# Three MLP chunks with summed weights: the engines' order written down in the source, the next item but one split into the buffers of the running one

## The chip, the cores and the metric

The kernel runs on one core of a Trainium2 chip. The metric is the device time of one execution in microseconds, the median of several runs; lower is better. Engine names are those of the profile: PE is TensorE (matmuls), PEld its weight loads, ACT is ScalarE, DVE is VectorE, SP issues the loads.

## The reference

One decoder layer on 256 tokens of width 2048: a recurrent branch and a windowed attention branch, an output projection, then a squared-ReLU MLP and a final norm. The change lies in the MLP alone:

```python
h2 = _modulate(_rms_norm(x, norm2_g[l]), shift2, scale2)
ff = jnp.square(jax.nn.relu(jnp.einsum("bsd,df->bsf", h2, w_ff1[l])))      # 2048 -> 8192
x = x + gate2[:, None, :] * jnp.einsum("bsf,fd->bsd", ff, w_ff2[l])        # 8192 -> 2048
return _rms_norm(x, final_g)
```

Inputs and outputs are float32.

## The kernel before

**Split operands.** Each matmul operand is held as a rounded part and a rest (`wh` and `wl` for weights), and three matmuls (wh by both parts of the activations, wl by the rounded part) stand for one product. A weight tile of 1 MB arrives in a buffer `raw` (in the profile `rw`); ACT rounds it into `wh` (`w_round`, L178) and DVE subtracts (`w_rest`, L183) into `wl`, in two pieces of 1024 columns. There are four `raw` buffers, four of `wh` and four of `wl`. So two items (a running one and the next) fill `wh` and `wl`, and the pieces of the next but one can only go where the running item's pieces were.

**Four chunks.** The hidden width of 8192 is cut in four chunks c = 0 to 3 of 16 tiles. In chunks 1 to 3, with which the change deals, three kinds of item follow each other on PE:

- **F items** (`ff1_unit`), 16 to a chunk: 48 matmuls of 128x256 (L204 to L206) into half of a PSUM bank; two F items that follow each other share a bank (`half_of`), from the fifth on. Then ACT applies relu (L1099), square (L1103) and rounds the result (L166), and DVE subtracts the rest (L167).
- **S items** (`sum_step`), 16 to a chunk: 21 matmuls (L1033 to L1035). They work out eight tiles of the second layer with 7 products of sums in the place of 8, as in Strassen's scheme. Their left side is a pair of F results and sums of its four blocks (`token_sums`: DVE L978 to L981 for every second F, then ACT L983 and DVE L984). Their right side is made by `weight_sums`: two loads (L991, 512 KB in all), three DVE sums in the same buffer (L993, L996, L997), and the same rounding and subtracting in pieces of 1024 and 768 columns.
- **G items** (`ff2_unit`): the other eight tiles of the second layer. Tiles 8 to 11 have 48 narrow matmuls into half banks; DVE adds each to the residual (L1209). Tiles 12 to 15 use a wide form (L229 and L230).

PE's order in such a chunk is F0 F1 F2 F3 S0 F4 S1 F5 ... F15 S12 G8 S13 G9 S14 G10 S15 G11 G12 and so on. During S14 and S15 the seven banks of the products become complete, and `sums_out` copies them out (c = 1, ACT L1008) or adds them to what the chunk before left (c = 2 and 3, DVE L1010). At the end of chunk 3 the products are joined (L1049), transposed back (L1056) and added to the residual.

**What sets the order.** A loop over all units asks, ahead of unit n, for loads and splits up to unit n + 2, then runs unit n. A scheduler turns that into the order on each engine while it builds the program; only instructions that are wrapped in `pin` keep the order of the source. Before the change, nothing of chunks 1 to 3 is pinned but the last two G tiles. Each engine works off its instructions in the order so made: one that waits holds back all behind it.

Of the kernel before, what the change touches and what calls it, by code (L numbers as in the profile page):

```python
# [10 lines left out]
F32 = mybir.dt.float32  # L11
# [6 lines left out]
P = 128  # L18
T = 256
# [47 lines left out]
def hybrid_layer(ctx: ExitStack, tc: tile.TileContext, x, xt, wada, w_p, w_r, w_f, vec, lruw, relb,  # L67
# [108 lines left out]
    def w_round(raw, o, c, pin=lambda i: i):  # L176
        wh = wp.tile([P, WCH], F32R, tag="wh", name=nm("wh"), bufs=WH_BUFS)
        pin(se.activation(wh[:, :c], raw[:, o:o + c], AF.Copy))  # L178
        return wh

    def w_rest(raw, o, c, wh, pin=lambda i: i):
        wl = wp.tile([P, WCH], F32R, tag="wl", name=nm("wl"), bufs=WH_BUFS)
        pin(ve.tensor_tensor(out=wl[:, :c], in0=raw[:, o:o + c], in1=wh[:, :c].bitcast(F32), op=ALU.subtract))  # L183
        return wh, wl
# [789 lines left out]
    def token_sums(p):  # L974
        a, b = sq.pop(2 * p), sq.pop(2 * p + 1)
        a11, a21, a12, a22 = a[:, :P], a[:, P:], b[:, :P], b[:, P:]
        s = tmp([P, 4, P])
        ve.scalar_tensor_tensor(out=s[:, 0], in0=a21, scalar=-1.0, in1=a22, op0=ALU.mult, op1=ALU.subtract)  # L978
        ve.scalar_tensor_tensor(out=s[:, 1], in0=s[:, 0], scalar=-1.0, in1=a11, op0=ALU.mult, op1=ALU.subtract)
        ve.tensor_tensor(out=s[:, 2], in0=a11, in1=a21, op=ALU.subtract)  # L980
        ve.tensor_tensor(out=s[:, 3], in0=a12, in1=s[:, 1], op=ALU.subtract)  # L981
        hi, lo = (kp.tile([P, 4, P], F32R, tag="k2", name=nm("ts")) for _ in range(2))
        se.activation(hi, s, AF.Copy)  # L983
        ve.tensor_tensor(out=lo, in0=s, in1=hi.bitcast(F32), op=ALU.subtract)  # L984
        ts[p] = hi, lo

    def weight_sums(u, p):
        raw = wp.tile([P, 8, T], F32, tag="raw", name=nm("rw"), bufs=RAW_BUFS)
        for k in range(2):
            e = (2 * p + k) * P  # L990
            nc.sync.dma_start(out=raw[:, 2 * k:2 * k + 2].rearrange("p a (b m) -> p (a b) m", m=P),  # L991
                              in_=w_f[u:u + SUMMED, :, e:e + P].rearrange("u p m -> p u m"))
        ve.tensor_tensor(out=raw[:, 4:6], in0=raw[:, 1:3], in1=raw[:, 0:1].broadcast_to((P, 2, T)), op=ALU.subtract)  # L993
        flat = raw.rearrange("p a b -> p (a b)")
        parts = [w_rest(flat, T, 4 * T, w_round(flat, T, 4 * T))]
        ve.tensor_tensor(out=raw[:, 6], in0=raw[:, 2], in1=raw[:, 4], op=ALU.add)  # L996
        ve.tensor_tensor(out=raw[:, 7], in0=raw[:, 6], in1=raw[:, 3], op=ALU.subtract)  # L997
        return parts + [w_rest(flat, 5 * T, 3 * T, w_round(flat, 5 * T, 3 * T))]

    yt = []  # L1000

# [15 lines left out]
    def sum_step(c, p, u, q):  # L1017
        def run(w):
            if p == 0 and q == 0:
                pq[0] = [bank([P, 2, T]) for _ in range(4)]  # L1020
                pq[0] += [pg.tile([P, 2, T], F32, tag="pg", name=nm("pg")) for _ in range(7 * QUADS // 2 - 4)]
            hi, lo = ts[p]
            fa, fb = ff[c, 2 * p], ff[c, 2 * p + 1]
            own = lambda f, t: (f[:, 0, t * P:(t + 1) * P], f[:, 1, t * P:(t + 1) * P])
            of = lambda i: (hi[:, i], lo[:, i])
            prods = ((own(fa, 0), 0, 0), (own(fb, 0), 0, 2), (of(3), 0, 1), (of(0), 0, 3),
                     (of(2), 1, 0), (of(1), 1, 1), (own(fb, 1), 1, 2))
            for n, ((xh, xl), i, o) in enumerate(prods, 7 * q):
# [4 lines left out]
                te.matmul(ps, lhsT=xh, rhs=wh[:, e], start=p == 0 and n % 2 == 0, stop=False)  # L1033
                te.matmul(ps, lhsT=xh, rhs=wl[:, e], start=False, stop=False)
                te.matmul(ps, lhsT=xl, rhs=wh[:, e], start=False, stop=end)  # L1035
# [4 lines left out]
        add_unit(run, lambda: weight_sums(u, p), 1024)  # L1040

    def joined(q, i):
        return yt[(7 * q + i) // 2][:, (7 * q + i) % 2]
# [27 lines left out]
    def half_of(f, own=False):  # L1071
        if own or f % 2 == 0:
            hb[0] = pg.tile([P, 2, T], F32, tag="pg", name=nm("pg"))
        return hb[0][:, f % 2]

    def ff1_unit(c, f):
        def run_first(w):
            ps = pg.tile([P, 258], F32, tag="pg", name=nm("pg"))
            for k in range(KT):
                wh, wl = w[k * P // WCH]  # L1080
                e = slice(k * P % WCH, k * P % WCH + P)
                te.matmul(ps, lhsT=wh[:, e], rhs=z[k][:, 0:258], start=k == 0, stop=False)  # L1082
# [12 lines left out]

        def run(w):
            t = tmp()
            if c >= SUMMED_FROM:
                se.activation(t[:, 0], gemm(w, 0, [zn[k] for k in range(KT)], half_of(f, f < 4)), AF.Relu)  # L1099
            else:  # L1100
                gemm_wide(w, [zn[k] for k in range(KT)], out=t[:, 0])
                se.activation(t[:, 0], t[:, 0], AF.Relu)
            se.activation(t[:, 1], t[:, 0], AF.Square)  # L1103
            ff[c, f] = split(t[:, 1])
            if c >= SUMMED_FROM:
                sq[f] = t[:, 1]
                if f % 2 == 1:
                    token_sums(f // 2)
        add_unit(run_first if c == 0 and f < ZN_FROM else run)

    def rest_part(f, w, acts):
# [81 lines left out]
    def ff2_unit(c, f):  # L1193
        def run(w):
            if c == 3 and f >= 14:
                held.append(w)
                if f == 15:
                    last_units(*held)
                return
            if c == 0:  # L1200
                flush(5 * KT + f + 1)
            acts = [ff[c, j] for j in range(16)]
            if c >= SUMMED_FROM and f < SUMMED * QUADS + 4:
                pss = [gemm(w, 0, acts, half_of(f))]
            else:
                ps = gemm_wide(w, acts, join=False)
                pss = [ps[:, 0], ps[:, 1]]
            for ps in pss:
                ve.scalar_tensor_tensor(out=x1[f], in0=ps, scalar=mod[:, 5 * KT + f:5 * KT + f + 1], in1=x1[f],  # L1209
                                        op0=ALU.mult, op1=ALU.add)  # L1210
# [28 lines left out]
    for c in range(4):  # L1239
        summed = SUMMED * QUADS if c >= SUMMED_FROM else 0  # L1240
        u2 = full[0] + 16
        steps = [(p, u2 + q * SUMMED, q) for p in range(KT // 2) for q in range(QUADS)] if summed else []
        for f in range(16):
            ff1_unit(c, f)
            if f > 2 and steps:
                sum_step(c, *steps.pop(0))
        full[0] += summed
        for f in range(summed, 16):
            ff2_unit(c, f)
            if steps:  # L1250
                sum_step(c, *steps.pop(0))

    ready, credit, ada_credit = {0: split_w.pop(len(p_units))}, 0.0, 0.0
    for n, (run, src, size) in enumerate(units):
        if n == ATT:
            stage[0] = pin
            attention(ready)
            stage[0] = same
        if ATT <= n < ATT + 2 * GROUPS:
            continue  # L1260
        left = n_z - n
        if n < n_ya:
# [116 lines left out]
```

## Time and profile before

| | |
|---|---|
| median of 3 runs | 1571.03 us (1569.51 to 1571.73) |
| the profiled execution: its time | 1570.03 us |
| its span | 1568.2 us |
| DVE busy in the span | 1302.1 us (83%) |
| ACT busy in the span | 923.7 us (59%) |
| relu of the 48 F items (L1099), first and last start | 1015.5 and 1499.0 us |

Times inside the span count from its start. The profile's parts that are used below are: the busy time of each engine in stretches of the span, with instruction counts in brackets; the list of waits (who waited, for whom, total us, times, longest); and the timeline (start, us, engine, line, operation, with the idle time ahead of it and what ended it in square brackets). An instruction may start a little ahead of the end of the one in front of it, so the distance between two starts, not the duration, is what an engine pays for it in a dense queue.

### The profile page before, as it was taken

To read this page: it belongs to the slowest core of one execution; us is meant where nothing else is said; L and a number is where in the kernel's file an instruction comes from. 1 tells how busy PE (TensorE), PEld (TensorE's weight loads), DVE (VectorE), ACT (ScalarE), POOL (GpSimd) and SP (SyncE) were. 2 spreads that over 40 slices of the span, in tenths; PEclk is the share of its full clock that TensorE was granted. 3 is DMA by queue.
4 is the path that set the end of the run, shared out by engine and by line. 5 is a ranking of instruction groups with operands and counts; after the bars stand their busy time and mean duration, and the time that the engine had idled before them with its cause. 6 is when DMAs were issued, how large, how long until landed. Compare 5 with 4: busy or idle time off the path is not lost.

```text
span 1568.2 us, 28025 instructions
## 1 busy us (share of the span) xinstructions
PE 1541.7 (98%) x11225; PEld 1444.7 (92%) x11225; DVE 1302.1 (83%) x2059; ACT 923.7 (59%) x1517; POOL 0.2 (0%) x4
## 2 busy tenths in 40 slices
PE   8999999999999999999999999999999999999998
PEld 7999999999988888888889988999999999999997
DVE  5898988889899899998898877877776777777887
ACT  5753456667998664444566853465554555456565
POOL 0000000000000000000000000000000000000000
PEclk9999999999999999999999999999999999999999
DMA  9998976665677769888877677845564555645561
GB/s 371 360 377 314 365 286 232 224 233 203 231 257 262 244 242 366 323 298 309 332 274 264 209 263 267 310 161 170 197 230 148 165 184 176 242 146 190 179 221 71
DMA packets 108370, 388.09 MB, mean 247 GB/s; under 512 B 7920, under 2 KB 61520, under 8 KB 69584
## 3 DMA queue, kind: packets, MB, share of 16 engines
q1 hardware_dynamic: 103248, 381.51, 67.7%
q10 hardware_dynamic: 4992, 4.79, 1.0%
q8 instruction: 88, 1.44, 0.4%
q14 instruction: 42, 0.34, 0.1%
HBM read 384.13 MB, written 2.15 MB: 246 GB/s over the span
## 4 chain that ended last, share of the span: by engine, by line
PE 77%; DVE 9%; DMA 8%; ACT 3%; issue 2%; SPq 0%; DVEq 0%; ACTq 0%
PE pg L230 24%; PE pg L229 11%; PE pg L204 10%; PE pg L206 10%; PE pg L205 10%; DMA rw<-in_w_f_dram 7%; DVE wl L183 6%; ACT wh L178 1%; PE pg L1084 1%; PE pg L1083 1%; PE pg L1082 1%; DMA ra<-in_wada_dram 1%; PE pg L232 1%; PE pa L678 1%; PE pa L725 1%
## 5 line engine op out<-in xcount | busy, mean ns | idle before, releaser
L178 ACT ACTIVATE wh<-rw 128x1024 fp32r<-128x1024 f32 (+2 forms) x566 | 575.8, 1029 | 404.4 <-PE pg L230 149.7
L183 DVE TENSOR_TENSOR wl<-rw,wh 128x1024 fp32r<-128x1024 f32 (+2 forms) x566 | 667.6, 1188 | 100.4 <-ACT wh L178 97.2
L230 PE MATMUL pg<-k,wh 128*128 128x512 f32 x1680 | 581.7, 394 | 0.7 <-DVE k L167 0.7
L206 PE MATMUL pg<-k,wl 128*128 128x256 f32 x1838 | 517.2, 282 | 10.1 <-DVE wl L183 9.5
L204 PE MATMUL pg<-k,wh 128*128 128x256 f32 x1838 | 518.9, 282 | 2.1 <-DVE k L1209 2.1
L205 PE MATMUL pg<-k,wh 128*128 128x256 f32 x1838 | 515.3, 280 | 0.0
L229 PE MATMUL pg<-k,wl 128*128 128x256 f32 x1575 | 441.7, 281 | 0.0
L230 PEld LDWEIGHTS pg<-k,wh 128*128 128x128 f32 x1680 | 308.9, 188 | 64.8 <-PE pg L230 0.9
L206 PEld LDWEIGHTS pg<-k,wl 128*128 128x128 f32 x1838 | 346.0, 188 | 14.7 <-DVE wl L183 14.4
L204 PEld LDWEIGHTS pg<-k,wh 128*128 128x128 f32 x1838 | 346.2, 188 | 7.4 <-issue 5.5
L205 PEld LDWEIGHTS pg<-k,wh 128*128 128x128 f32 x1838 | 345.8, 188 | 0.3
L229 PEld LDWEIGHTS pg<-k,wl 128*128 128x128 f32 x1575 | 296.1, 188 | 5.4 <-ACT k L166 0.8
L283 DVE CUSTOM_DVE_ANT_0 ra<-ra,scr,vc 128x2048 f32<-128x2048 f32 x96 | 225.1, 2345 | 10.0 <-DMA ra<-in_wada_dram 8.6
L993 DVE TENSOR_TENSOR rw<-rw 128x512 f32<-128x512 f32 x48 | 33.2, 692 | 86.3 <-DMA rw<-in_w_f_dram 86.3
L983 ACT ACTIVATE ts<-t 128x512 fp32r<-128x512 f32 x24 | 15.2, 634 | 80.8 <-DVE t L981 80.8
L236 ACT ACTIVATE t<-pg 128x256 f32<-128x256 f32 x79 | 28.9, 366 | 24.4 <-PE pg L230 24.4
L686 ACT ACTIVATE t<-t,as 128x128 f32<-128x128 f32 x64 | 28.4, 445 | 22.4 <-DVE as L683 22.4
L1082 PE MATMUL pg<-z,wh 128*128 128x258 f32 x144 | 40.9, 284 | 0.0
L1083 PE MATMUL pg<-z,wh 128*128 128x256 f32 x144 | 40.9, 284 | 0.0
L1084 PE MATMUL pg<-z,wl 128*128 128x258 f32 x144 | 40.7, 283 | 0.0
L1209 DVE SCALAR_TENSOR_TENSOR k<-pg,mod,k 128x256 f32<-128x256 f32 x64 | 30.8, 481 | 10.9 <-PE pg L230 7.6
L167 DVE TENSOR_TENSOR k<-t,k 128x256 fp32r<-128x256 f32 x80 | 33.5, 420 | 3.9 <-ACT k L166 3.9
(237 smaller groups left out, 1636.4 us busy)
## 6 DMA issues: line engine op xcount, KB each, us to landing
rw<-in_w_f_dram SPq DMA_DIRECT2D x176, 1024.0 KB, 5.0
ra<-in_wada_dram SPq DMA_DIRECT2D x96, 1024.0 KB, 6.6
rw<-in_w_r_dram SPq DMA_DIRECT2D x30, 1024.0 KB, 5.2
rw<-in_w_p_dram SPq DMA_DIRECT2D x29, 960.0 KB, 7.1
rw<-in_w_f_dram SPq DMA_DIRECT2D x96, 256.0 KB, 3.2
bt<-ud ACTq DMA_DIRECT2D x8, 512.0 KB, 3.6
k<-in_w_p_dram SPq DMA_DIRECT2D x9, 256.0 KB, 10.8
lw<-in_lruw_dram SPq DMA_DIRECT2D x4, 512.0 KB, 6.2
```

The lines of the kernel that those rows point to most:

```text
L167: pin(ve.tensor_tensor(out=hl[:, 1], in0=src, in1=hl[:, 0].bitcast(F32), op=ALU.subtract))
L178: pin(se.activation(wh[:, :c], raw[:, o:o + c], AF.Copy))
L183: pin(ve.tensor_tensor(out=wl[:, :c], in0=raw[:, o:o + c], in1=wh[:, :c].bitcast(F32), op=ALU.subtract))
L204: pin(te.matmul(ps, lhsT=wh[:, w], rhs=hl[:, 0], start=k == 0, stop=False))
L205: pin(te.matmul(ps, lhsT=wh[:, w], rhs=hl[:, 1], start=False, stop=False))
L206: pin(te.matmul(ps, lhsT=wl[:, w], rhs=hl[:, 0], start=False, stop=k == n - 1))
L229: te.matmul(ps[:, 0], lhsT=wl[:, w], rhs=hl[:, 0], start=False, stop=False)
L230: te.matmul(ps, lhsT=wh[:, w], rhs=hl, start=k == 0, stop=k == n - 1)
L283: pin(ve.tensor_tensor_reduce(out=raw, in0=raw, in1=scr, scale=1.0, scalar=vc[:, V_BADA + c:V_BADA + c + 1], op0=ALU.mult, op1=ALU.add, ac ...
L1082: te.matmul(ps, lhsT=wh[:, e], rhs=z[k][:, 0:258], start=k == 0, stop=False)
L1083: te.matmul(ps[:, 0:256], lhsT=wh[:, e], rhs=z[k][:, 258:514], start=False, stop=False)
L1084: te.matmul(ps, lhsT=wl[:, e], rhs=z[k][:, 0:258], start=False, stop=k == KT - 1)
```

## The change

The order of SP, ACT, DVE and PE in chunks 1 to 3 is written out, from the chunk's first F item to S15, with `pin` around every instruction. Items become objects with `ask` (loads), `sum`, `round` and `rest`, and `mlp` walks over them. While item i runs, item i + 2 is rounded and split (into the buffers that i frees), the sums of an S item at i + 3 are made if i is not an S item, and after it the loads of item i + 6 are asked for. The part of `token_sums` that rounds and splits (`token_parts`) moves behind the splits of the item that follows. What is computed stays the same.

```diff
-    def weight_sums(u, p):
-        raw = wp.tile([P, 8, T], F32, tag="raw", name=nm("rw"), bufs=RAW_BUFS)
-        for k in range(2):
...
-        ve.tensor_tensor(out=raw[:, 4:6], in0=raw[:, 1:3], in1=raw[:, 0:1].broadcast_to((P, 2, T)), op=ALU.subtract)
-        flat = raw.rearrange("p a b -> p (a b)")
-        parts = [w_rest(flat, T, 4 * T, w_round(flat, T, 4 * T))]
-        ve.tensor_tensor(out=raw[:, 6], in0=raw[:, 2], in1=raw[:, 4], op=ALU.add)
-        ve.tensor_tensor(out=raw[:, 7], in0=raw[:, 6], in1=raw[:, 3], op=ALU.subtract)
-        return parts + [w_rest(flat, 5 * T, 3 * T, w_round(flat, 5 * T, 3 * T))]
+    class Item:
...
+        def sum(self):
+            r = self.sums
+            pin(ve.tensor_tensor(out=r[:, 4:6], in0=r[:, 1:3], in1=r[:, 0:1].broadcast_to((P, 2, T)), op=ALU.subtract))
+            pin(ve.tensor_tensor(out=r[:, 6], in0=r[:, 2], in1=r[:, 4], op=ALU.add))
+            pin(ve.tensor_tensor(out=r[:, 7], in0=r[:, 6], in1=r[:, 3], op=ALU.subtract))
...
+    def mlp(items, ready, n):
+        items[0].parts, items[1].parts = ready[n], ready[n + 1]
+        end = len(items) - 2
+        for it in items[2:6]:
+            it.ask()
+        late = []
+        for i, it in enumerate(items[:end]):
+            new, soon = items[i + 2], items[i + 3] if i + 3 < len(items) else None
+            ps = it.run(it.parts)
+            ready[n + i] = it.parts = None
+            new.round()
+            new.rest()
+            if not it.step and soon and soon.step:
+                soon.sum()
+            if not it.step:
+                it.done[0](ps)
+            new.round()
+            if not it.step:
+                it.done[1](ps)
+            new.rest()
+            if not it.step:
+                it.done[2](ps)
+            while late:
+                token_parts(*late.pop(0))
+            if it.done and it.done[3]:
+                late.append((it.done[3][0], token_sums(it.done[3][0])))
+            if i + 6 < len(items):
+                items[i + 6].ask()
...
+    def first_item(c, f):
+        t = {}
+        def relu(ps):
+            t[0] = tmp()
+            pin(se.activation(t[0][:, 0], ps, AF.Relu))
...
+        return Item(run, (relu, square, rest, [f // 2] if f % 2 else None), next_src())
+    def second_item(c, f):
+        def out(ps):
+            pin(ve.scalar_tensor_tensor(out=x1[f], in0=ps, scalar=mod[:, 5 * KT + f:5 * KT + f + 1], in1=x1[f],
+                                        op0=ALU.mult, op1=ALU.add))
...
+        return Item(run, (same, same, out, None), next_src())
...
+        if n in pinned:
+            mlp(pinned[n], ready, n)
-        if ATT <= n < ATT + 2 * GROUPS:
+        if ATT <= n < ATT + 2 * GROUPS or n in inside:
             continue
```

The order on SP is the same before and after, row by row, and so is all that stands ahead of chunk 1 on every engine; PE's differs only in where the transposes of chunk 3 stand. What moves is the order on DVE and ACT in the three chunks.

On DVE, the first place is the alternation of F and S items in chunk 1. The names carry the buffers' numbers: SP loads rw1738, rw1750, rw1758, rw1763, rw1773 in this order (S, F, S, F, S), and with four buffers rw1773 goes where rw1738 was. Before:

```order
L183 TENSOR_TENSOR wl1742_11207<-rw1738_11195,wh1741_11205 128x768
L984 TENSOR_TENSOR ts1737_11192<-t1735_11186,ts1736_11191 128x512
L183 TENSOR_TENSOR wl1752_11241<-rw1750_11237,wh1751_11239 128x1024
L993 TENSOR_TENSOR rw1773_11410<-rw1773_11410 128x512
L183 TENSOR_TENSOR wl1754_11245<-rw1750_11237,wh1753_11243 128x1024
L996 TENSOR_TENSOR rw1773_11410<-rw1773_11410 128x256
L183 TENSOR_TENSOR wl1760_11308<-rw1758_11302,wh1759_11306 128x1024
L167 TENSOR_TENSOR k1757_11299<-t1755_11247,k1757_11299 128x256
L183 TENSOR_TENSOR wl1762_11314<-rw1758_11302,wh1761_11312 128x768
L997 TENSOR_TENSOR rw1773_11410<-rw1773_11410 128x256
L183 TENSOR_TENSOR wl1765_11341<-rw1763_11337,wh1764_11339 128x1024
```

After, at the like place, SP loads rw1711, rw1720, rw1730, rw1739, rw1753 (S, F, S, F, S), and rw1753 goes where rw1711 was:

```order
L183 TENSOR_TENSOR wl1750_11238<-rw1711_10985,wh1749_11236 128x768
L987 TENSOR_TENSOR ts1752_11241<-t1738_11197,ts1751_11240 128x512
L183 TENSOR_TENSOR wl1756_11298<-rw1720_11059,wh1755_11296 128x1024
L1010 TENSOR_TENSOR rw1730_11128<-rw1730_11128 128x512
L1011 TENSOR_TENSOR rw1730_11128<-rw1730_11128 128x256
L1012 TENSOR_TENSOR rw1730_11128<-rw1730_11128 128x256
L183 TENSOR_TENSOR wl1760_11310<-rw1720_11059,wh1758_11305 128x1024
L1146 TENSOR_TENSOR k1759_11307<-t1757_11303,k1759_11307 128x256
L183 TENSOR_TENSOR wl1763_11338<-rw1730_11128,wh1762_11336 128x1024
L183 TENSOR_TENSOR wl1765_11342<-rw1730_11128,wh1764_11340 128x768
L183 TENSOR_TENSOR wl1768_11397<-rw1739_11202,wh1767_11395 128x1024
L1010 TENSOR_TENSOR rw1753_11244<-rw1753_11244 128x512
```

The three sums L993, L996 and L997 are now L1010 to L1012, the rest of `token_sums` L984 is now L987, and L167 of the F results is L1146. Between the last reading of a buffer's old contents and the first sum on what is loaded into it next stood two rows; now ten stand there, and the three sums lie together ahead of their own splits.

The second place is DVE in chunk 2 around the end of G9, whose residual update writes k1335 (L1209, now L1154); `scr` with `pa` is the first addition of finished products (in the source before L1010, now L1063). Before:

```order
L997 TENSOR_TENSOR rw2216_14740<-rw2216_14740 128x256
L183 TENSOR_TENSOR wl2213_14685<-rw2211_14681,wh2212_14683 128x1024
L1209 SCALAR_TENSOR_TENSOR k1335_8614<-pg2205_14596,mod_107,k1335_8614 128x256
L1010 TENSOR_TENSOR scr_104<-pa2025_13310,scr_104 128x512
L183 TENSOR_TENSOR wl2215_14689<-rw2211_14681,wh2214_14687 128x1024
```

After:

```order
L183 TENSOR_TENSOR wl2216_14740<-rw2196_14558,wh2215_14738 128x1024
L1010 TENSOR_TENSOR rw2203_14593<-rw2203_14593 128x512
L1011 TENSOR_TENSOR rw2203_14593<-rw2203_14593 128x256
L1012 TENSOR_TENSOR rw2203_14593<-rw2203_14593 128x256
L1063 TENSOR_TENSOR scr_104<-pa2022_13305,scr_104 128x512
L183 TENSOR_TENSOR wl2218_14747<-rw2196_14558,wh2217_14745 128x1024
L1154 SCALAR_TENSOR_TENSOR k1335_8614<-pg2204_14596,mod_107,k1335_8614 128x256
```

The update of G9 stood ahead of the second split of G10 (rw2211) and of the first addition of products; now it stands behind both (rw2196 is G10's).

More of the change, by code (lines that the diff above doesn't have):

```diff
@@ L977, in token_sums @@
         s = tmp([P, 4, P])
[L978 to L981, printed above, removed]
+        pin(ve.scalar_tensor_tensor(out=s[:, 0], in0=a21, scalar=-1.0, in1=a22, op0=ALU.mult, op1=ALU.subtract))
@@ L982, in token_sums, with token_parts @@
+        pin(ve.scalar_tensor_tensor(out=s[:, 1], in0=s[:, 0], scalar=-1.0, in1=a11, op0=ALU.mult, op1=ALU.subtract))
+        pin(ve.tensor_tensor(out=s[:, 2], in0=a11, in1=a21, op=ALU.subtract))
+        pin(ve.tensor_tensor(out=s[:, 3], in0=a12, in1=s[:, 1], op=ALU.subtract))
+        return s
+    def token_parts(p, s):
         hi, lo = (kp.tile([P, 4, P], F32R, tag="k2", name=nm("ts")) for _ in range(2))
-        se.activation(hi, s, AF.Copy)
-        ve.tensor_tensor(out=lo, in0=s, in1=hi.bitcast(F32), op=ALU.subtract)
+        pin(se.activation(hi, s, AF.Copy))
+        pin(ve.tensor_tensor(out=lo, in0=s, in1=hi.bitcast(F32), op=ALU.subtract))
@@ L985, in token_sums, with __init__, ask, round @@
         ts[p] = hi, lo
-    def weight_sums(u, p):
-        raw = wp.tile([P, 8, T], F32, tag="raw", name=nm("rw"), bufs=RAW_BUFS)
-        for k in range(2):
[L990 to L993, printed above, removed]
-        flat = raw.rearrange("p a b -> p (a b)")
-        parts = [w_rest(flat, T, 4 * T, w_round(flat, T, 4 * T))]
-        ve.tensor_tensor(out=raw[:, 6], in0=raw[:, 2], in1=raw[:, 4], op=ALU.add)
-        ve.tensor_tensor(out=raw[:, 7], in0=raw[:, 6], in1=raw[:, 3], op=ALU.subtract)
-        return parts + [w_rest(flat, 5 * T, 3 * T, w_round(flat, 5 * T, 3 * T))]
+    class Item:
+        def __init__(self, run, done, src=None, u=None, p=None):
+            self.run, self.done, self.src, self.u, self.p = run, done, src, u, p
+            self.step = src is None
+            self.cuts = ((T, 4 * T), (5 * T, 3 * T)) if self.step else ((0, WCH), (WCH, WCH))
+            self.whs, self.parts = [], []
+        def ask(self):
+            if not self.step:
+                self.raw = w_dma(self.src, 2048, pin)[0]
+                return
+            self.sums = wp.tile([P, 8, T], F32, tag="raw", name=nm("rw"), bufs=RAW_BUFS)
+            for k in range(2):
+                e = (2 * self.p + k) * P
+                pin(nc.sync.dma_start(out=self.sums[:, 2 * k:2 * k + 2].rearrange("p a (b m) -> p (a b) m", m=P),
+                                      in_=w_f[self.u:self.u + SUMMED, :, e:e + P].rearrange("u p m -> p u m")))
+            self.raw = self.sums.rearrange("p a b -> p (a b)")
+        def sum(self):
[3 more added lines that the diff above has]
+            pin(ve.tensor_tensor(out=r[:, 7], in0=r[:, 6], in1=r[:, 3], op=ALU.subtract))
+        def round(self):
+            self.whs.append(w_round(self.raw, *self.cuts[len(self.whs)], pin))
+        def rest(self):
+            j = len(self.parts)
+            self.parts.append(w_rest(self.raw, *self.cuts[j], self.whs[j], pin))
@@ new lines, in mlp @@
+    def mlp(items, ready, n):
[26 more added lines that the diff above has]
+                items[i + 6].ask()
+        while late:
+            token_parts(*late.pop(0))
+        ready[n + end], ready[n + end + 1] = items[end].parts, items[end + 1].parts
@@ L1032, in run @@
                 end = p == KT // 2 - 1 and n % 2 == 1
-                te.matmul(ps, lhsT=xh, rhs=wh[:, e], start=p == 0 and n % 2 == 0, stop=False)
-                te.matmul(ps, lhsT=xh, rhs=wl[:, e], start=False, stop=False)
-                te.matmul(ps, lhsT=xl, rhs=wh[:, e], start=False, stop=end)
+                pin(te.matmul(ps, lhsT=xh, rhs=wh[:, e], start=p == 0 and n % 2 == 0, stop=False))
+                pin(te.matmul(ps, lhsT=xh, rhs=wl[:, e], start=False, stop=False))
+                pin(te.matmul(ps, lhsT=xl, rhs=wh[:, e], start=False, stop=end))
             if q == QUADS - 1:
@@ L1039, in run @@
                     sums_out(c)
-        add_unit(run, lambda: weight_sums(u, p), 1024)
+        chunk[-1][1].append(Item(run, None, u=u, p=p))
+        add_unit(run, lambda: None, 1024)
     def joined(q, i):
@@ L1074, in half_of, with square, rest, run @@
         return hb[0][:, f % 2]
+    chunk = []
+    def first_item(c, f):
[3 more added lines that the diff above has]
+            pin(se.activation(t[0][:, 0], ps, AF.Relu))
+        def square(_):
+            hl = ff[c, f] = pair(F32R)
+            pin(se.activation(t[0][:, 1], t[0][:, 0], AF.Square))
+            pin(se.activation(hl[:, 0], t[0][:, 1], AF.Copy))
+        def rest(_):
+            sq[f] = t[0][:, 1]
+            pin(ve.tensor_tensor(out=ff[c, f][:, 1], in0=sq[f], in1=ff[c, f][:, 0].bitcast(F32), op=ALU.subtract))
+        def run(w):
+            return gemm(w, 0, [zn[k] for k in range(KT)], half_of(f, f < 4), pin)
+        return Item(run, (relu, square, rest, [f // 2] if f % 2 else None), next_src())
[3 more added lines that the diff above has]
+                                        op0=ALU.mult, op1=ALU.add))
+            if c == 3:
+                last_square(f)
+        def run(w):
+            return gemm(w, 0, [ff[c, j] for j in range(16)], half_of(f), pin)
+        return Item(run, (same, same, out, None), next_src())
+    def next_src():
+        return w_f[full[0]]
     def ff1_unit(c, f):
@@ L1097, in run @@
             t = tmp()
[L1098 to L1102, printed above, removed]
+            gemm_wide(w, [zn[k] for k in range(KT)], out=t[:, 0])
+            se.activation(t[:, 0], t[:, 0], AF.Relu)
             se.activation(t[:, 1], t[:, 0], AF.Square)
             ff[c, f] = split(t[:, 1])
[L1105 to L1108, printed above, removed]
+        if c >= SUMMED_FROM:
+            chunk[-1][1].append(first_item(c, f))
         add_unit(run_first if c == 0 and f < ZN_FROM else run)
@@ L1212, in run @@
                 last_square(f)
+        if c >= SUMMED_FROM and f < SUMMED * QUADS + 5:
+            chunk[-1][1].append(second_item(c, f))
         add_unit(run)
@@ L1242, in hybrid_layer @@
         steps = [(p, u2 + q * SUMMED, q) for p in range(KT // 2) for q in range(QUADS)] if summed else []
+        if summed:
+            chunk.append((len(units), []))
         for f in range(16):
@@ L1251, in hybrid_layer @@
                 sum_step(c, *steps.pop(0))
+    pinned = dict(chunk)
+    inside = set()
+    for n, items in chunk:
+        inside.update(range(n, n + len(items) - 2))
     ready, credit, ada_credit = {0: split_w.pop(len(p_units))}, 0.0, 0.0
```

## The prediction

> **What bounds the kernel now.** I read the page first, for the span and for PE's share; then the busy times by stretch, to see where PE falls behind its pace; then the waits there; then the timeline, for the loop behind them.
>
> ```profile
> span 1568.2 us, 28025 instructions
> PE 1541.7 (98%) x11225; PEld 1444.7 (92%) x11225; DVE 1302.1 (83%) x2059; ACT 923.7 (59%) x1517; POOL 0.2 (0%) x4
> ...
> rw<-in_w_f_dram SPq DMA_DIRECT2D x176, 1024.0 KB, 5.0
> ```
>
> PE is busy for 98% of the span, so the kernel is bound by PE, and a change of order can win only what PE loses by waiting. Where that is, the stretches show. The first is a stretch of six S and F pairs in chunk 1 that runs smoothly; the others begin where chunks 1, 2 and 3 begin to lose pace, and end with the first matmul after G9.
>
> ```profile
> core 0: us, PE busy (x) PEld busy (x) DVE busy (x) ACT busy (x) POOL busy (x), PEclk, DMA share, GB/s
> 1031.49:1080.45 48.96, 48.96 (x417) 48.96 (x416) 39.43 (x63) 30.26 (x45) 0.00 (x0) 1.00 0.54 175
> 1082.94:1153.06 70.12, 64.74 (x534) 63.18 (x533) 52.96 (x84) 36.73 (x54) 0.00 (x0) 1.00 0.52 169
> 1249.52:1335.78 86.26, 81.99 (x672) 79.80 (x671) 66.59 (x105) 46.87 (x69) 0.00 (x0) 1.00 0.53 174
> 1440.40:1515.68 75.28, 72.78 (x602) 71.35 (x602) 59.20 (x93) 43.28 (x64) 0.00 (x0) 1.00 0.56 180
> ```
>
> The counts hold two or three matmuls that began ahead of the edge. Six pairs are 6 x (48 + 21) = 414 matmuls in 48.96 us, a pace of 0.1183 us, 5.68 us for an F and 2.48 us for an S, 8.16 us a pair. At that pace 531, 669 and 600 matmuls take 62.8, 79.1 and 71.0 us; the stretches took 70.1, 86.3 and 75.3. PE loses 7.3 + 7.1 + 4.3 = **18.7 us** here. The granted clock is 1.00 throughout. More than these 18.7 us the change can't win.
>
> ```profile
> DVE rw L993 <- DMA rw<-in_w_f_dram: 86.3, 45, 4.0
> ...
> PEld pg L206 <- DVE wl L183: 14.4, 22, 1.7
> ```
>
> PE's weight loads wait for the rest `wl` (22 times, 14.4 us; with the slower restarts the larger part of the 18.7), and DVE, which makes it, stands for 86.3 us before the first sum L993 until a load lands. One turn of this:
>
> ```profile
> 1080.05 0.92 SPq L991 DMA_DIRECT2D rw<-in_w_f_dram  x2
> ```
>
> ```profile
> 1085.45 0.69 DVE L993 TENSOR_TENSOR rw<-rw 128x512 f32<-128x512 f32 x1 [3.96 <-DMA rw<-in_w_f_dram]
> 1086.06 1.22 DVE L183 TENSOR_TENSOR wl<-rw,wh 128x1024 fp32r<-128x1024 f32 x1
> 1087.20 0.28 DVE L978 SCALAR_TENSOR_TENSOR t<-t,t 128x128 f32<-128x128 f32 x1
> 1087.40 0.28 DVE L980 TENSOR_TENSOR t<-t 128x128 f32<-128x128 f32 x1
> 1087.60 0.28 DVE L979 SCALAR_TENSOR_TENSOR t<-t,t 128x128 f32<-128x128 f32 x1
> 1087.81 1.22 DVE L183 TENSOR_TENSOR wl<-rw,wh 128x1024 fp32r<-128x1024 f32 x1
> 1088.94 0.42 DVE L167 TENSOR_TENSOR k<-t,k 128x256 fp32r<-128x256 f32 x1
> 1089.28 0.28 DVE L981 TENSOR_TENSOR t<-t,t 128x128 f32<-128x128 f32 x1
> 1089.48 0.95 DVE L183 TENSOR_TENSOR wl<-rw,wh 128x768 fp32r<-128x768 f32 x1
> 1090.35 0.69 DVE L984 TENSOR_TENSOR ts<-t,ts 128x512 fp32r<-128x512 f32 x1
> 1090.95 0.42 DVE L996 TENSOR_TENSOR rw<-rw 128x256 f32<-128x256 f32 x1
> 1091.29 1.22 DVE L183 TENSOR_TENSOR wl<-rw,wh 128x1024 fp32r<-128x1024 f32 x1
> ```
>
> An S buffer is asked for at 1080.05, as soon as it is free; DVE stops at 1085.45 - 3.96 = 1081.49 and holds back two F splits until the load is in, 5.40 us after its issue. Then it works 4.90 us (1085.45 to 1090.35) until the next S buffer is free. 5.4 + 4.9 us is a turn of 10.3 us where the load takes long, against PE's 8.16. In the smooth stretch the loads still run ahead.
>
> **The change, part by part.** Loads, splits, sums and matmuls keep their number and size, so nothing is removed or added but waits.
>
> *The S sums move.* By the order of after, ten DVE rows lie between the freeing of an S buffer and its next first sum, where two did: 0.60 + 1.14 + 1.29 + 1.14 + 0.34 + 1.14 + 0.87 + 1.14 = 7.7 us of work, by the distances of the starts above (the three sums as 0.61 + 0.34 + 0.34). That alone is over the 5.4 us of the load. To see whether something else is late, I walk one pair, F at 0, for ACT with these rows:
>
> ```profile
> 1036.54 0.63 ACT L983 ACTIVATE ts<-t 128x512 fp32r<-128x512 f32 x1 [1.24 <-DVE t L981]
> 1037.08 1.04 ACT L178 ACTIVATE wh<-rw 128x1024 fp32r<-128x1024 f32 x1
> 1039.68 1.06 ACT L178 ACTIVATE wh<-rw 128x1024 fp32r<-128x1024 f32 x1 [1.56 <-PE pg L205]
> 1040.64 0.36 ACT L1099 ACTIVATE t<-pg 128x256 f32<-128x256 f32 x1
> 1041.04 0.42 ACT L1103 ACTIVATE t<-t 128x256 f32<-128x256 f32 x1
> 1041.36 1.04 ACT L178 ACTIVATE wh<-rw 128x1024 fp32r<-128x1024 f32 x1
> 1042.31 0.40 ACT L166 ACTIVATE k<-t 128x256 fp32r<-128x256 f32 x1
> 1042.62 0.83 ACT L178 ACTIVATE wh<-rw 128x768 fp32r<-128x768 f32 x1
> ```
>
> F frees its first `wh` piece with its 23rd matmul, at 22 x 0.118 + 0.28 = 2.88. ACT rounds there for the next F until 3.94; DVE splits and sums from 3.96 to 6.39. F ends at 5.84: relu, second rounding until 7.27, square and copy until 7.82. DVE: second split from 7.30, rest of F's result from 8.44, token sums (every second F) until 9.58. S frees its pieces at 7.2 and 8.3; ACT rounds for the next S until 8.88 and 9.61; DVE splits from 9.58 to 11.59, and makes the token rest until 12.19. The next first split of an F could start at 3.96 + 8.16 = 12.12. So a pair with tokens overruns by 0.07 us, the pair without them (0.80 + 0.60 less) has over 1 us to spare, and nothing piles up. PE needs the next F's second piece at 8.16 + 24 x 0.118 = 11.0 (there at 8.5) and the next S at 13.8 (there at 10.8): 2.5 us or more in hand. An F load is issued at 8.4, an S load at 11.6; they are used at 19.2 and 21.4 (two pairs on), 10.8 and 9.8 us for loads of 5.0 and 5.4. **The F and S pairs run at PE's pace.**
>
> *The G items get the wait instead.* Before, it was there once in a chunk, at G9:
>
> ```profile
> 1146.67 0.47 DVE L1209 SCALAR_TENSOR_TENSOR k<-pg,mod,k 128x256 f32<-128x256 f32 x1
> 1147.26 0.19 PEld L204 LDWEIGHTS pg<-k,wh 128*128 128x128 f32 x1 [0.86 <-ACT wh L178]
> 1147.30 0.36 PE L204 MATMUL pg<-k,wh 128*128 128x256 f32 x1 [0.68 <-DVE k L1209]
> ...
> 1147.50 0.28 PE L205 MATMUL pg<-k,wh 128*128 128x256 f32 x1
> ```
>
> G9 starts 0.16 us after the update of G8 ends (1147.14), though it writes the other half of the bank; with 0.86 us of idle weight loads (put down to ACT there; the matmul's row names the update) and 0.08 for the slow first matmul this costs 0.94 us, 2.8 in three chunks, which leaves 15.9 us of the 18.7 for the pairs. [...]
>
> In the new order the update stands behind the second split of item i + 2, which must wait for the end of the G: with the end of its 48 places at 0, rounding 0.04 to 1.08, split at 1.10, update at 2.24 to 2.71, first matmul at 2.87, where PE could start after S at 2.48. That is 0.39 + 0.08 = 0.47 us at G9, and as much at G10 (with three product tiles and its own, all four `pg` banks are taken) and at G11. In chunks 2 and 3 an addition of products is ahead of the split:
>
> ```profile
> 1516.69 0.68 DVE L1010 TENSOR_TENSOR scr<-pa,scr 128x512 f32<-128x512 f32 x1
> ```
>
> It is followed 0.60 us later. At G10 it waits for six matmuls of S14 (5 x 0.118 + 0.28, so 0.92), the split starts at 1.52, the update ends at 3.13, PE starts at 3.29: 0.89 us. At G11 it waits for three of S15 and costs 0.54. Sum: 3 x 0.47 in chunk 1, 0.47 + 0.89 + 0.54 in each of the other two, **5.2 us** where 2.8 were. The bounds: nothing (2.8 won), or the 0.94 of now at all nine (8.5).
>
> *The end of chunk 3.* The same additions, joins and transposes shift against the splits of G12 and G13; I put this at nothing, since PE has G11 and G12 (5.7 us each) as cover, with 1 us either way where a transpose meets a late join.
>
> **Sum.** -15.9 - 2.8 + 5.2 = -13.5 us. The profiled execution took 1570.03, so 1556.5; it lies 1.0 under the median of 1571.03, from which the sum is 1557.5. I say **1557**.
>
> **The rivals.**
>
> *Everything goes.* If the updates come in time at the G items too, 18.7 us: 1551 to 1552. For it: only 0.4 us is missing at most of the nine. Against: the row at 1147.30.
>
> *Half of the stalls stay.* The pair with tokens has no room on DVE. If a few waits in the queue take some tenths more, half of 15.9 us may stay: 1565. For it: DVE can't pass a row that waits. Against: 2.5 us in hand at each use.
>
> *The loads are the limit, and the order doesn't matter.* Then only the G items change, +2.4: 1573. Against: the loads use 0.52 to 0.56 of the DMA engines in the stretches, at 169 to 180 GB/s, and only the buffers' freeing decides when they start.
>
> *Slower: DVE becomes the bound.* A row of DVE that follows another engine's work may cost its duration and a hand-over, not the distance of starts. By durations the walk above takes 8.96 us with tokens (2.44 and 2.17 for the splits, 1.53 for the sums, 0.42, 1.12 and 0.69 for result and tokens, 0.59 of waiting for the second rounding) and 7.15 without, 8.06 in the mean. With 0.12 us (1147.14 to 1147.26, from DVE to PE's load) at each of the 6.5 rows in a pair that follow another engine, it is 8.84, 0.68 over PE's 8.16. With 13 pairs a chunk, 39 in all, this is 26.5 us where 15.9 are lost now: with the G items 1583. It is slower from 0.41 us a pair on (15.9 / 39), a hand-over of 0.08. Against: the splits above follow roundings too, and the next row starts 1.13 to 1.14 after them.
>
> **How the numbers follow.** Forecast 0.60 (1553 to 1561, from the bounds of the G items and the end), everything goes 0.10, half stays 0.15, loads 0.07, slower 0.08. The range takes in the first three: 1551 to 1566, with some 0.17 left out. A measurement here can tell 0.2% (3.1 us) from no change: faster 0.85 (the first three), within 0.2% 0.07 (loads), slower 0.08.
>
> **What would show it.** Right: the wait of the first S sum for its load is gone or under 10 us in all; weight loads of F items no longer wait for `wl`; the three stretches run at 0.118 us a matmul up to G9; at G9, G10 and G11 PE waits for the update, 0.4 to 0.9 us each. Wrong: DVE dense at over 95% in these stretches with PE waiting for `wl` (DVE is the bound), or SP's loads landing later than two pairs after their issue. What would make it wrong most easily is a DVE row that waits for ACT longer than I counted.

## The result and the profile after

| | before | after |
|---|---|---|
| median of the runs beside each other (us) | 1571.38 (4 runs, 1569.51 to 1572.10) | 1558.06 (4 runs, 1556.84 to 1558.68) |
| profiled execution, and its span (us) | 1570.03, 1568.2 | 1556.84, 1555.0 |

The changed kernel takes 0.9916 of the time, with a 95% interval of 0.9899 to 0.9933. It was forecast at 1557.0; of the profiled execution the working had said 1556.5, and it took 1556.84. So close an agreement is in part chance: the executions of one kernel lie some 2 us apart.

The head of the page of the changed kernel:

```profile
span 1555.0 us, 28010 instructions
...
PE 1536.9 (99%) x11225; PEld 1443.4 (93%) x11225; DVE 1314.1 (85%) x2059; ACT 928.0 (60%) x1517; POOL 0.2 (0%) x4
```

The work is the same (11225 matmuls, 2059 instructions on DVE), in 13.2 us less. Next come the busy times by stretch. The three stretches hold the same matmuls as the last three shown of before (531, 669 and 600, up to the first matmul after G9); their edges are the times at which these begin and end in this trace.

```profile
core 0: us, PE busy (x) PEld busy (x) DVE busy (x) ACT busy (x) POOL busy (x), PEclk, DMA share, GB/s
1082.92:1146.16 63.24, 62.95 (x533) 62.77 (x532) 54.00 (x82) 37.91 (x53) 0.00 (x0) 1.00 0.63 205
1243.67:1323.37 79.70, 79.38 (x671) 79.21 (x670) 68.01 (x103) 48.16 (x68) 0.00 (x0) 1.00 0.63 203
1429.75:1501.14 71.39, 71.09 (x603) 70.92 (x601) 60.40 (x90) 43.43 (x62) 0.00 (x0) 1.00 0.59 194
```

They took 70.12, 86.26 and 75.28 us and take 63.24, 79.70 and 71.39: 17.3 us less, and 0.4 to 0.6 us each above the pace of PE. DVE is busy for 85% of each. The DMA engines carry more a microsecond than before (0.59 to 0.63 of them busy, 0.52 to 0.56 then), since the same loads go through in less time: the loads had not been a limit.

One turn of the pairs on DVE, in the timeline of the changed kernel (start, duration, engine, line, operation; in brackets the idle time ahead and what ended it):

```profile
1087.02 1.22 DVE L183 TENSOR_TENSOR wl<-rw,wh 128x1024 fp32r<-128x1024 f32 x1
1088.15 0.69 DVE L1010 TENSOR_TENSOR rw<-rw 128x512 f32<-128x512 f32 x1
1088.87 0.42 DVE L1011 TENSOR_TENSOR rw<-rw 128x256 f32<-128x256 f32 x1
1089.33 0.43 DVE L1012 TENSOR_TENSOR rw<-rw 128x256 f32<-128x256 f32 x1
1090.17 1.23 DVE L183 TENSOR_TENSOR wl<-rw,wh 128x1024 fp32r<-128x1024 f32 x1 [0.41 <-ACT wh L178]
1091.31 0.42 DVE L1146 TENSOR_TENSOR k<-t,k 128x256 fp32r<-128x256 f32 x1
```

The first sum (L993 of before, now L1010) starts 1.13 us after the row ahead of it and waits for nothing; before, it had 3.96 us of waiting at the like place. The view of L1010 by itself says the same for all 48: it lists no idle time ahead of them, where before 45 of 48 waited 86.3 us. DVE still waits, but now for ACT's rounding. The row of that wait from 1005 to 1530 in the changed kernel:

```profile
DVE wl L183 <- ACT wh L178: 84.9, 93, 2.2
```

and in the kernel before:

```profile
DVE wl L183 <- ACT wh L178: 30.3, 29, 1.7
```

DVE's waits for loads and rounding together went only from 116.6 to 84.9 us. What changed is that they no longer hold PE up: DVE is ahead and waits for ACT, and ACT for PE (82.4 us for a free `wh`, 91.2 us for the result of an F item).

The waits of PE in chunks 1 to 3 (from 1005 to 1530), all that the view has:

```profile
engine line waited for: us in total, times, longest us
PE pg L204 <- DVE k L1154: 3.5, 9, 0.7
```

In the same stretch of the kernel before, that view has

```profile
PE pg L206 <- DVE wl L183: 9.5, 12, 1.5
PE pg L204 <- DVE k L1209: 2.1, 3, 0.7
```

so PE waited for the rests `wl` and three times for the update. Now its matmuls wait only for the update, nine times: at G9, G10 and G11. G9 in chunk 1, with the first row of S13, the update of G8 and what is queued around it:

```profile
1137.47 0.29 PE L1086 MATMUL pa<-wh,k 128*128 128x256 f32 x1
...
1138.64 1.23 DVE L183 TENSOR_TENSOR wl<-rw,wh 128x1024 fp32r<-128x1024 f32 x1
...
1139.79 0.48 DVE L1154 SCALAR_TENSOR_TENSOR k<-pg,mod,k 128x256 f32<-128x256 f32 x1
...
1140.41 0.36 PE L204 MATMUL pg<-k,wh 128*128 128x256 f32 x1 [0.29 <-DVE k L1154]
...
1146.16 0.28 PE L1086 MATMUL pa<-wh,k 128*128 128x256 f32 x1
```

S13 begins at 1137.47 and would end its 2.48 us at 1139.95. G9 begins at 1140.41, 0.46 us late, 0.14 us after the update ends; and G9 itself takes 5.75 us where 5.68 is its pace, because its first matmul is slow (0.20 us from its start to the next one's, not 0.12). The update is late since the split ahead of it in the queue, which waits for the end of the G item, takes DVE from 1138.64 to 1139.87. In chunk 2, at G10, the addition of products stands ahead of that split as well:

```profile
1323.37 0.28 PE L1086 MATMUL pa<-wh,k 128*128 128x256 f32 x1
...
1324.41 0.68 DVE L1063 TENSOR_TENSOR scr<-pa,scr 128x512 f32<-128x512 f32 x1
...
1325.01 1.22 DVE L183 TENSOR_TENSOR wl<-rw,wh 128x1024 fp32r<-128x1024 f32 x1
...
1326.14 0.48 DVE L1154 SCALAR_TENSOR_TENSOR k<-pg,mod,k 128x256 f32<-128x256 f32 x1
...
1326.76 0.36 PE L204 MATMUL pg<-k,wh 128*128 128x256 f32 x1 [0.74 <-DVE k L1154]
```

S14 has 3.39 us between its start and the next item's, 0.91 over its pace.

### The profile page after: what moved, and what is told of

It is laid out like the page before. It is cut to its first block, busy times and chain, and to the rows that moved or that the text cites. A ratio compares the mean times of both kernels' runs of the same rounds, so it can differ in the third digit from the quotient of the medians.

```text
span 1555.0 us, 28010 instructions
## 1 busy us (share of the span) xinstructions
PE 1536.9 (99%) x11225; PEld 1443.4 (93%) x11225; DVE 1314.1 (85%) x2059; ACT 928.0 (60%) x1517; POOL 0.2 (0%) x4
## 4 chain that ended last, share of the span: by engine, by line
PE 91%; ACT 3%; DVE 3%; DMA 2%; issue 1%; SPq 0%; DVEq 0%; ACTq 0%
PE pg L230 23%; PE pg L204 14%; PE pg L205 13%; PE pg L206 13%; PE pg L229 11%; DMA ra<-in_wada_dram 2%; ACT wh L178 1%; PE pa L1086 1%; PE pa L1088 1%; PE pa L1087 1%; DVE wl L183 1%; PE pg L1174 1%; PE pg L1173 1%; PE pg L1172 1%; PE pg L1087 1%
## 5 line engine op out<-in xcount | busy, mean ns | idle before, releaser
L1137 ACT ACTIVATE t<-pg 128x256 f32<-128x256 f32 x48 | 18.5, 385 | 91.2 <-PE pg L206 91.2
L236 ACT ACTIVATE t<-pg 128x256 f32<-128x256 f32 x79 | 29.0, 367 | 24.1 <-PE pg L230 24.1
L237 DVE TENSOR_TENSOR t<-pg,t 128x256 f32<-128x256 f32 x79 | 33.0, 418 | 2.6 <-ACT t L236 2.6
L1294 DVE SCALAR_TENSOR_TENSOR k<-pg,mod,k 128x256 f32<-128x256 f32 x55 | 26.5, 482 | 10.0 <-PE pg L230 7.7
L1010 DVE TENSOR_TENSOR rw<-rw 128x512 f32<-128x512 f32 x48 | 32.9, 685 | 0.0
```

The source lines that it names most:

```text
L237: ve.tensor_tensor(out=t, in0=ps[:, 0], in1=t, op=ALU.add)
```

## The experiments

By their labels, in two sets; the runs of one set share a chip and the runs of the kernel before (1569.64 median of 7 runs with the first, 1571.06 of 9 with the second). "Loss" is the time of the F, S and G8 to G11 items of chunks 1 to 3 over their pace, summed from the starts of their first matmuls; it is 18.7 us before and 5.1 after.

| label | set | median (us) | ratio to before, 95% | loss (us) |
|---|---|---|---|---|
| e1_update_first | 1 | 1552.88 | 0.9891 (0.9873 to 0.9910) | -0.2 |
| e2_sums_pair_earlier | 1 | 1641.76 | 1.0455 (1.0438 to 1.0471) | 88.6 |
| e3_sums_half_pair_earlier | 1 | 1558.05 | 0.9925 (0.9910 to 0.9940) | 4.9 |
| e5_before_sums_pinned | 1 | 1555.34 | 0.9908 (0.9892 to 0.9924) | 3.0 |
| e4_tokens_at_once | 2 | 1560.74 | 0.9932 (0.9914 to 0.9951) | 8.0 |
| e6_after_beside | 2 | 1557.62 | 0.9912 (0.9898 to 0.9926) | 5.1 |
| e7_update_first_beside | 2 | 1551.88 | 0.9875 (0.9859 to 0.9890) | -0.2 |

**Is the place of the update what costs the time at the G items?** In the changed kernel the update of a G item is moved ahead of the second rounding and split of item i + 2:

```diff
-        return Item(run, (same, same, out, None), next_src())
+        return Item(run, (out, same, same, None), next_src())
```

> After, with one thing moved: the residual update of G8, G9 and G10 stands on DVE ahead of the second split of the next item but one, no longer behind it. Theory (PE waits at G9, G10 and G11 for the update of the G before, 5.1 us in all, because the two share a PSUM bank or the last free one): the update then starts 0.2 us after the G ends and is done at about 0.7, where PE needs it at 2.48; the waits of PE for the update go to zero, and the time falls by 4 to 5 us, to about 1553.5. Rival (the row names the update, but the split of the next G is what comes late, since it is due at the same time): the wait stays under another name and the time stays at 1558.

The same place as above, in this kernel's timeline:

```profile
1139.99 0.48 DVE L1154 SCALAR_TENSOR_TENSOR k<-pg,mod,k 128x256 f32<-128x256 f32 x1
1140.39 2.52 DVE L183 TENSOR_TENSOR wl<-rw,wh 128x1024 fp32r<-128x1024 f32 x2
```

The update ends at 1140.47, and the first matmul of G9 starts at 1141.40, one place of 0.12 us behind the last of S13. The waits of PE from 1005 to 1530 are an empty list, and PE is busy without a break:

```profile
1005.00:1530.00 525.00, 525.00 (x4273) 516.95 (x4272) 428.50 (x634) 307.97 (x437) 0.00 (x0) 1.00 0.58 190
```

The loss of 5.1 us is gone. That the bank is shared by the update and the next item's matmuls stayed as it was; the place in the queue alone decided whether this costs anything. All four `pg` banks are in use there, so that no run shows what a bank of its own for G9 would give.

The two medians of this kernel lie 16.8 us (here) and 19.2 us (`e7_update_first_beside`) under that of before. Its profiled span here is 16.9 us shorter, not the full 18.9 that the loss went down by, since in this execution chunk 1 begins at 1010.19 where it began at 1008.74 before, and the part behind G11 takes 36.6 us where it took 36.1.

**Does the distance between the freeing of a buffer and the first sum decide?** The sums are put a whole pair earlier, close behind the split that frees their buffer (one F split lies between, in every second pair a token rest as well); all else stays as in the changed kernel:

```diff
-            new, soon = items[i + 2], items[i + 3] if i + 3 < len(items) else None
+            new, soon = items[i + 2], items[4 if i == 0 else i + 5] if i + 5 < len(items) else None
```

> After, with one thing moved: the three sums of an S item stand one pair (F and S) earlier on DVE, as far ahead of their splits as before the change, directly behind the freeing of the buffer they work in. Everything else keeps the written order. Theory (the position of the first sum is what starved PE before): DVE stops at each first sum for most of a load of 4 to 5.4 us, a turn of DVE takes about 9 to 10.5 us against PE's 8.16, and once the loads' lead is used up PE loses 1 to 2 us a pair: 15 to 60 us over the time of after, 1573 or more. Rival (the gain came from the written order of ACT and of the splits, and the sums' place is a side issue): under 4 us over after.

The waits between 1005 and 1540, the first and those of PE:

```profile
DVE rw L1010 <- DMA rw<-in_w_f_dram: 116.0, 42, 4.9
...
PEld pg L206 <- DVE wl L183: 52.4, 30, 2.9
PE pg L206 <- DVE wl L183: 46.2, 30, 2.7
PE pg L204 <- DVE k L1154: 11.4, 6, 5.0
```

Three successive first sums, with the issue of the load that the second one waits for:

```profile
1122.25 0.69 DVE L1010 TENSOR_TENSOR rw<-rw 128x512 f32<-128x512 f32 x1 [2.05 <-DMA rw<-in_w_f_dram]
...
1133.37 0.69 DVE L1010 TENSOR_TENSOR rw<-rw 128x512 f32<-128x512 f32 x1 [4.90 <-DMA rw<-in_w_f_dram]
...
1143.44 0.69 DVE L1010 TENSOR_TENSOR rw<-rw 128x512 f32<-128x512 f32 x1 [2.32 <-DMA rw<-in_w_f_dram]
```

```profile
1127.37 0.92 SPq L1004 DMA_DIRECT2D rw<-in_w_f_dram  x2
```

Turns of 11.1 and 10.1 us (10.0 in the mean, from the third turn of a chunk on), against PE's 8.16: the loop of before (free, load, wait, work, free) is back, and stronger. DVE stops 1.1 us after the issue of the load (at 1133.37 - 4.90 = 1128.47), in the turns with a token rest 1.7 us after it; in the kernel before that was 1.4 us (1081.49 against 1080.05) to 2.4. It costs 1.2 to 2.5 us in nearly every pair from the third of a chunk on, where before it set in only in mid-chunk, when the lead of the loads had been used up. And it costs at the G items, where the update now stands behind a waiting sum: PE waits 5.0 us at G9. So the direction is as forecast, but the size is 84 us over the changed kernel. One part of it was not thought of at all, and stands at the end of this document.

**Is it a threshold?** The sums are put half a pair earlier, so that more rows lie between than in the last kernel and fewer than in the changed one:

```diff
-            new, soon = items[i + 2], items[i + 3] if i + 3 < len(items) else None
+            new, soon = items[i + 2], items[i + 4] if i + 4 < len(items) else None
...
+            if soon and soon.step and (it.step or i == 0 or i == 2):
+                soon.sum()
             new.round()
             new.rest()
-            if not it.step and soon and soon.step:
-                soon.sum()
```

> After, with the three sums of an S item half a pair earlier: at the head of DVE's work for the S item before, not in the middle of that for the F item between. Theory (a stall begins only where the first sum comes before the load has landed): the buffer is free at 11.6 us of the pair, the load is in by 17.0, and the sum now comes at 17.7 in place of 21.4; 0.7 us in hand, so the time stays within 2 us of after, 1556 to 1560, with a few short waits of the sum for the load. Rival (each earlier place costs in proportion): about half of what a whole pair costs, 8 us or more over after.

Of the waits, those of the sums and of PE:

```profile
DVE rw L1010 <- DMA rw<-in_w_f_dram: 9.0, 12, 3.6
...
PE pg L204 <- DVE k L1154: 3.3, 9, 0.6
```

Twelve sums wait again, and PE loses nothing by it: its only waits are the nine for the update, and the loss is that of the changed kernel. The longest wait, 3.6 us, stands ahead of the first S item of chunk 1; between the first S item and 1498 none is over 0.6. DVE came to the first sum 5.1 us after the load's issue (1080.84 to 1085.95) or 3.7 us after it (1089.59 to 1093.29), and neither of these two had to wait. So a stall on DVE costs PE nothing here where it is short or stands alone; in the kernel with the sums a whole pair earlier it came back each turn, before DVE had made up what it had lost.

**Is the whole written order needed?** In the kernel before, the scheduler stays in charge, and only the three sums and the two splits of an S item are pinned, in this order, the sums ahead:

```diff
-        ve.tensor_tensor(out=raw[:, 4:6], in0=raw[:, 1:3], in1=raw[:, 0:1].broadcast_to((P, 2, T)), op=ALU.subtract)
         flat = raw.rearrange("p a b -> p (a b)")
-        parts = [w_rest(flat, T, 4 * T, w_round(flat, T, 4 * T))]
-        ve.tensor_tensor(out=raw[:, 6], in0=raw[:, 2], in1=raw[:, 4], op=ALU.add)
-        ve.tensor_tensor(out=raw[:, 7], in0=raw[:, 6], in1=raw[:, 3], op=ALU.subtract)
-        return parts + [w_rest(flat, 5 * T, 3 * T, w_round(flat, 5 * T, 3 * T))]
+        pin(ve.tensor_tensor(out=raw[:, 4:6], in0=raw[:, 1:3], in1=raw[:, 0:1].broadcast_to((P, 2, T)), op=ALU.subtract))
+        pin(ve.tensor_tensor(out=raw[:, 6], in0=raw[:, 2], in1=raw[:, 4], op=ALU.add))
+        pin(ve.tensor_tensor(out=raw[:, 7], in0=raw[:, 6], in1=raw[:, 3], op=ALU.subtract))
+        return [w_rest(flat, o, n, w_round(flat, o, n), pin) for o, n in ((T, 4 * T), (5 * T, 3 * T))]
```

> The kernel before, with one part of the change alone: the three sums of an S item stand together directly ahead of its two splits, and these five DVE instructions keep the order of the source; ACT, PE, the F items and the tokens stay with the scheduler. Theory (the place of the sums alone starved PE): the wait of the first sum for its load goes from 86 us to under 10, and most of the 15.9 us that the pairs lost goes; since ACT can now round an S item only behind its sums, DVE waits about 1 us a pair there, and 0 to 6 us may stay. 10 to 16 us under the time of before, 1555 to 1561. Rival (the whole written order is needed): under 4 us gained.

Here the update of a G item is L1208. The waits of PE from 1005 to 1530:

```profile
PE pg L204 <- DVE k L1208: 2.8, 3, 0.9
PE pg L232 <- DVE wl L183: 0.5, 1, 0.5
```

No first sum waits for its load any more, and of the 18.7 us lost, 3.0 are left, at G9 alone (1.0 to 1.1 in each chunk). So five pinned instructions give all that the change won in the pairs. They don't leave the rest as it was: the scheduler placed other rows anew around them (the two splits of an F item now follow those of S at once, four in a row), so that this kernel shows how little has to be pinned, not the effect of moving the sums and nothing else. G10 and G11 cost nothing, because the scheduler has the update ahead of the split there, as it had before. The median is 2.7 us under that of the half-pair kernel of the same set, which loses what the changed kernel loses; the intervals of their ratios overlap, so that one isn't shown to be faster than the other.

**Was ACT's waiting for the token sums a cause of its own?** Before, ACT had waited for them too. In the changed kernel the tokens are rounded and split as soon as they are summed, not one item later:

```diff
-                late.append((it.done[3][0], token_sums(it.done[3][0])))
+                token_parts(it.done[3][0], token_sums(it.done[3][0]))
```

> After, with one thing put back: the rounding and the rest of the token sums follow them at once, ahead of the splits of the S item that comes next, no longer behind them. Theory (their late place is of little weight): ACT holds back the rounding for the next S item by about 2.4 us in every second pair and DVE's splits of it by 1.8, against 3 us in hand, and the pair without tokens has 1.3 us to catch up the overrun of 1.2; 0 to 2 us over after. Rival (ACT's 81 us of waiting for the token sums before the change was part of the stall, and the late place is what freed it): 5 us or more over after.

Of the waits between 1005 and 1540:

```profile
ACT ts L986 <- DVE t L981: 43.3, 24, 1.8
...
PE pg L204 <- DVE k L1154: 6.7, 9, 1.4
```

ACT waits 43.3 us for the tokens, and the pairs lose nothing by it. The 3 us that this kernel is slower than the changed one beside it arise elsewhere: at G9, where the loss is 1.51 us in each chunk in place of 0.46. The queue of DVE ahead of it:

```profile
1134.91 0.69 DVE L987 TENSOR_TENSOR ts<-t,ts 128x512 fp32r<-128x512 f32 x1 [0.70 <-ACT ts L986]
1135.87 3.23 DVE L183 TENSOR_TENSOR wl<-rw,wh 128x1024 fp32r<-128x1024 f32 x3 [0.26 <-ACT wh L178]
1139.01 0.69 DVE L1010 TENSOR_TENSOR rw<-rw 128x512 f32<-128x512 f32 x1
...
1141.67 0.48 DVE L1154 SCALAR_TENSOR_TENSOR k<-pg,mod,k 128x256 f32<-128x256 f32 x1
```

The last tokens before G8 (those of F15) hold DVE back for 0.70 us, and ACT's next roundings stand behind their rounding, so that DVE waits again for 0.26; all that follows, the update of G8 with it, is later by about 1 us. In the pairs the same delay has cover; at G9 there is none.

**The faster version against the changed kernel, side by side.** The changed kernel again, and that with the update first, with five rounds each on one chip:

> The changed kernel itself, as the mark for the others of this call: 1556 to 1560.

> The kernel with the update of the G items ahead of the second split, beside the changed kernel on the same chip. Theory: 4 to 5 us under it, the 5.1 us that PE waits at the nine G items, with the intervals of the two apart. Rival (no real difference): within 2 us.

1557.62 (1556.92 to 1558.45) against 1551.88 (1551.48 to 1552.07): 5.7 us less, and the intervals of their ratios (0.9898 to 0.9926 and 0.9859 to 0.9890) don't meet. It is the fastest kernel of this study.

## Why the prediction was right

*The bound.* Of the 18.7 us that PE lost in chunks 1 to 3, the kernel with the update first wins all: its loss is -0.2, which is nothing within the reading, and its medians are 16.8 and 19.2 us under those of before beside it. So no other limit shows up behind this one in the three chunks.

*The pairs at PE's pace* (15.9 us to win). Shown: no first sum waits, no weight load of an F item waits for `wl`, and the three stretches took 17.3 us less. The prediction's terms give the same for them: 15.9, and three times 0.94 - 0.47 at G9. The walk came out row by row on DVE: with an F item's first matmul at 1074.75, its second split starts 7.25 us later (7.30 in the walk), the token sums end at 9.66 (9.58), the splits for S at 11.66 (11.59), and the token rest at 12.27 (12.19); the first sums come 9.7 and 10.5 us after the issue of their loads (9.8). That it is the distance between the freeing of the buffer and the sum that matters, two kernels show in which only the sums move: 1.1 to 1.7 us of work between them bring the loss back, half a pair doesn't. A third, the old kernel with the sums and their splits pinned, wins it without the written order.

*The G items* (2.8 would become 5.2). They became 5.1: 0.46 us at each of the three in chunk 1, 0.46, 0.91 and 0.46 in chunk 2, 0.46 and 0.88 at G9 and G10 of chunk 3, and 0.07 more for the slow first matmul of each item. The walk had said 0.47, 0.89 and 0.54, each with 0.08 for the slow matmul in it; in these terms 0.53, 0.96 to 1.00, and 0.53 were measured. At G11 of chunk 3 two transposes come first; on the timeline of the changed kernel they and the first matmul of G11 read

```profile
1512.73 0.38 PE L1110 MATMUL pa<-idt,scr 128*128 128x128 f32 x2
1513.30 0.36 PE L204 MATMUL pg<-k,wh 128*128 128x256 f32 x1 [0.19 <-DVE k L1154]
```

so that some 0.4 us is lost there too: 5.5 in all, where 5.2 was forecast. 18.7 - 5.5 = 13.2 is the whole difference of the spans, and chunk 1 begins at the same time in both (1008.7). So the *end of chunk 3* came out at nothing, as put.

*The rivals.* "Everything goes" was wrong for this change and right for it with one tuple in another order; the forecast had seen that only 0.4 us was missing at most of the nine places. "DVE becomes the bound" fell: in the pairs DVE's rows follow each other at the distances read before, behind a split that had waited for a rounding too (1090.17 to 1091.31 is 1.14 us), and DVE is 85% busy, not dense. "The loads are the limit" fell with the first sums, of which none waits any more: the same bytes went through in 17 us less. "Half of the stalls stay" fell with the empty list of waits for `wl`.

*Two sizes in the experiments were off.* The sums a whole pair earlier cost 84 us, where 15 to 60 were expected. The turn was right (10.0 us, 9 to 10.5 expected); but the stall was put only where the loads' lead is used up, as before, and it comes in nearly every pair, catches the G items as well, and slows PE's clock (next but one section), the last for about 10 us of the 84: some 105 matmuls 0.21 us apart in place of 0.118. And the tokens at once cost 3.1 us at G9, between the two theories' numbers; neither had looked at what follows the tokens there.

## What to carry to other kernels

On an engine that takes its rows in order, find the first row that reads a fresh load and count the work between it and the row that freed the buffer: if that work is longer than the load (7.7 against 5.4 us here), the load is hidden, and if it is much shorter (1.1 to 1.7 us in the kernel with the sums a whole pair earlier), the engine stops nearly every turn and all behind it is late. Pinning those few rows (five here) may give the whole gain of an order written out for all engines, and such an order has to be read at the seams between kinds of items, where a short row that the next item waits for (the update, 0.4 us) can land behind a long one that is not urgent. A stall matters by its length against the lead of its engine at that place: 43 us of waits were free in the pairs, and 1 us at G9 was paid in full.

## What the runs showed of the hardware that was not expected

In the kernel with the sums a whole pair earlier, the granted clock falls to half at long waits of PE (0.50 from 1165.95 to 1170.50, by the busy times of that stretch). The longest of chunk 1, at G9, and the matmuls at its end:

```profile
1166.63 0.55 PE L204 MATMUL pg<-k,wh 128*128 128x256 f32 x1 [4.98 <-DVE k L1154]
1166.98 0.41 PE L205 MATMUL pg<-k,wh 128*128 128x256 f32 x1
1167.19 0.41 PE L206 MATMUL pg<-k,wl 128*128 128x256 f32 x1
```

After this wait of 4.98 us the matmuls stand 0.21 us apart, not 0.118, until 1171.67, and G9 takes 8.03 us in place of 5.68: the wait costs 2.35 us more than it lasts. It is so at G9 of each chunk (8.03, 7.94 and 7.66 us, 6.6 us over the pace together).

Shorter waits can do it too (2.22 us in one case), and their length alone doesn't decide. Here are two waits of nearly the same length, one in chunk 1 and one in chunk 2, and then for each of them the 3.41 us in which most of it lies and the 3.41 us behind (columns as in the stretches above; the granted clock is the third figure from the end):

```profile
1094.97 0.39 PE L206 MATMUL pg<-k,wl 128*128 128x256 f32 x1 [2.24 <-DVE wl L183]
...
1342.43 0.58 PE L206 MATMUL pg<-k,wl 128*128 128x256 f32 x1 [2.22 <-DVE wl L183]
```

```profile
1093.23:1096.64 3.41, 1.67 (x14) 1.67 (x15) 3.34 (x9) 0.42 (x1) 0.00 (x0) 1.00 0.26 38
1096.64:1100.06 3.42, 3.42 (x32) 3.42 (x31) 3.29 (x4) 3.31 (x7) 0.00 (x0) 1.00 0.80 315
...
1338.99:1342.40 3.41, 1.22 (x11) 1.01 (x9) 2.71 (x5) 0.00 (x0) 0.00 (x0) 1.00 0.00 0
1342.40:1345.81 3.41, 3.38 (x16) 3.39 (x17) 3.38 (x8) 1.58 (x2) 0.00 (x0) 0.50 0.65 223
```

The first leaves the clock at 1.00, the second is followed by 0.50. What makes the difference between these two is not settled here. In chunks 1 to 3 the kernel before (longest wait of PE there 1.5 us) and the changed one (0.7) stay at 1.00.
